# Values of the retention heads transposed by DMA as two 16-bit planes, and an order for ScalarE behind the second quad

## The chip, the cores and the metric

The kernel runs on one core of a Trainium2 chip. The metric is the time of one execution on the device in microseconds (us); the kernel is run several times and the median is given. The engines are TensorE (PE, with its weight loads as PEld), VectorE (DVE), ScalarE (ACT), GpSimd (POOL) and SyncE (SP), whose queue here issues all the transfers; 16 DMA engines carry them out.

## The reference

A decoder layer of 2048 positions and width 1024 with 16 learned meta tokens ahead of them. After an RMS norm, one projection gives eight groups of 512 columns. Four of them feed a gated short convolution, four (Q, K, V and a gate RG) feed four retention heads of width 128, computed in chunks of 128 positions:

```python
hn = rms_norm(h, norm_g)
cx, cb, cc, cg, q, k, v, rg = jnp.split(hn @ w_in, 8, axis=-1)
conv_out = short_conv(cx, cb, cc) * silu(cg)
scores = einsum('bhnid,bhnjd->bhnij', qc, kc) * decay
inner = einsum('bhnij,bhnje->bhnie', scores, vc)
upd = einsum('bhnjd,bhnje->nbhde', kc * zeta, vc)      # summed over positions
states: s = chunk_decay * s + upd                      # carried from chunk to chunk
cross = einsum('bhnid,nbhde->bhnie', qc * xi, states)
ret = head_group_norm(inner + cross) * silu(rg)
out = rms_norm(h + concat(conv_out, ret) @ w_out)
```

Both `inner` and `upd` sum over positions of a chunk, so V is needed with positions in the partitions. The projection leaves it with the head's 128 columns in the partitions.

## The kernel before

The 2048 positions are taken in two halves of 1024 (r = 0 and 1), each half in two blocks of 512 (j = 0 and 1). A half runs through eight units: 0 to 3 are the retention heads (`head`), 4 to 7 the convolution groups; the first half begins with group 4, then come heads 0 to 3. After both halves, `output` makes eight pairs of row tiles with the output projection.

Each unit has two quads of projections. A quad multiplies a 2x2 block of weights by a 2x2 block of activations in seven products instead of eight (`quad`); every factor is split into a high and a low part (`wh`, `wl` for weights, `mh`, `ml` for activations), so a product is 12 matmuls of 128x512. Products share banks of PSUM (`pj`): ACT copies a bank to `tc` after products 0, 2 and 3, and `take(i, j, bank, c)` hands the results over in the order (0,0), (1,1), (0,1), (1,0); the last one has no copy to be added. The weights of a quad are four loads `ra`; `stationary` builds the sums on POOL (first `sa`, of the last two loads, then three in place), casts on ACT (`wh`) and subtracts on DVE (`wl`), in a ring of three. The first quads of the program and the first of head 0 in the second half are plain ones of eight products (`quad_plain`), which hand over K and V of one j together.

A head's first quad gives K and V. K goes through `rotary` on DVE; V of j = 1 comes as the sum of a bank and a copy on DVE (L587 of the listing, shown as L110 in rows), V of j = 0 as a plain copy by ACT (L585). The second quad gives Q and RG. Then, for each j: four transposes of K on PE (L631) into a bank `ms`, scaled by ACT into `kd` (L633); four transposes of V on PE (L636) into another `ms`, scaled by four instructions of ACT, one a chunk, back into V's tile (L640); four update matmuls (L646) and four state updates on DVE (L649). Later stand the scores (L659), the two matmuls of the output (L669, L670), statistics on DVE, the power `rp` on POOL (L682), `pm` on DVE (L686), four transposes on PE (L693) and the store to `mixed` (L444).

Beside the heads run other pieces. After heads 1 and 2 of the first half, `prepare` makes the block sums of the second half's activations (`x`, L174 and L177, stored as `sums_x`); in the second half it does the same for the output weights. `prepared` loads these sums again as `t` (L200): eight of them between the two quads of head 0 in the second half, for products 3 and 4 of its second quad. `meta_state` loads a small table `mr` (L415) and sets the head's first state from the meta tokens (`mk`, L403, L425).

The order of instructions on each engine is set by the framework's scheduler, not by the order of the code alone; all transfers go through SP's queue in its order. Tiles named `kv`, `qg`, `x`, `t` come from one pool of 16 buffers (`gen`).

Of the kernel before, what the change touches and what calls it, by code (L numbers as in the profile page):

```python
# [8 lines left out]
F32 = mybir.dt.float32  # L9
F32R = mybir.dt.float32r  # L10
BF16 = mybir.dt.bfloat16
AF = mybir.ActivationFunctionType
ALU = mybir.AluOpType

P = 128
# [6 lines left out]
HB = 512  # L22
NR = 2
BLK = SEQ // NR
CH = HB // P
# [45 lines left out]
def hybrid_trunk(ctx: ExitStack, tc: tile.TileContext, t, out: bass.AP, chunk_decay):  # L71
# [5 lines left out]
    nc = tc.nc  # L77
# [11 lines left out]
    def ps_misc():  # L89
        return ps.tile([P, HB], F32, name="ms", tag="ms", bufs=4)  # L90

    def gen(name="g"):
        return sb.tile([P, HB + 16], F32, name=name, tag="g", bufs=GEN)[:, : 2 + HB]
# [99 lines left out]
    def prepared(m, src, ns, held={}):  # L193

        for n in ns:
            for kt in range(KH):
# [3 lines left out]
                    nc.sync.dma_start(a, src[n, kt])  # L200
                parts(m, SUMS[n], kt, a)

    def quad(w, m, take):


        def product(i, bank, first):
            (wh, wl) = w[i]
            for kt in range(KH):
                ks = slice(kt * P, (kt + 1) * P)
                mh, ml = m[i][kt]  # L210
                for n, (a, b) in enumerate(((wl, mh), (wh, ml), (wh, mh))):
                    nc.tensor.matmul(  # L212
                        bank, a[:, ks], b, start=first and kt == 0 and n == 0, stop=kt == KH - 1 and n == 2,
                        skip_group_check=not first,
                    )

        def copy(bank):
            c = sb.tile([P, HB], F32, name="tc", tag="tc", bufs=COPIES)
            nc.scalar.copy(out=c, in_=bank)  # L219
            return c  # L220

        xb = ps_proj()
        product(0, xb, True)
        c = copy(xb)
        yb = ps_proj()
        product(1, yb, True)
        take(0, 0, yb, c)
        product(2, xb, False)
        u2 = copy(xb)
        zb = ps_proj()  # L230
        product(3, zb, True)
        c = copy(zb)
        product(4, xb, False)
        take(1, 1, xb, c)
        product(5, zb, False)
        take(0, 1, zb, u2)
        product(6, xb, False)
        take(1, 0, xb, None)
# [61 lines left out]
    ident = const.tile([P, P], F32, name="ident")  # L300
# [265 lines left out]
    def rotary(a, table):  # L566
# [5 lines left out]
        nc.vector.tensor_tensor(out=a, in0=a, in1=table[:, 0, :], op=ALU.mult)  # L572
        turned[0] = nc.vector.tensor_tensor(out=a, in0=a, in1=rot[:, :w], op=ALU.add)

    def head(h, r, m, rot_t, f, blocks, ahead, first=(), between=()):


        between = iter(between)
        k, v = [None, None], [None, None]
        tables = [rot_t[:, :, j * HB : (j + 1) * HB] for j in range(2)]  # L580

        def take(i, j, pp, c):
            d = gen("kv")[:, :HB]
            if c is None:
                nc.scalar.copy(out=d, in_=pp)  # L585
            else:
                add(nc.vector, d, pp, c)  # L587
            if i == 0:
                rotary(d, tables[j])
                k[j] = d  # L590
            else:
                v[j] = d

        if len(first) > 0:
            quad_plain(first[0], m, take)
# [29 lines left out]
        blocks = ahead()  # L625
        states = [state[h]]
        vt = []
        for j in range(2):
            tp = ps_misc()
            for c in range(CH):  # L630
                nc.tensor.transpose(tp[:, c * P : (c + 1) * P], k[j][:, c * P : (c + 1) * P], ident)  # L631
            kd = brief("kd")
            nc.scalar.mul(kd, tp, kd_col[:, h : h + 1])  # L633
            tp = ps_misc()
            for c in range(CH):
                nc.tensor.transpose(tp[:, c * P : (c + 1) * P], v[j][:, c * P : (c + 1) * P], ident)  # L636
            vj = v[j]
            for c in range(CH):
                cs = slice(c * P, (c + 1) * P)
                nc.scalar.mul(vj[:, cs], tp[:, cs], f[2][j][0][:, c : c + 1])  # L640
            vt.append(vj)
            last = r == NR - 1 and j == 1
            up = ps_misc()
            for c in range(CH - last):
                cs = slice(c * P, (c + 1) * P)
                nc.tensor.matmul(up[:, cs], kd[:, cs], vj[:, cs], start=True, stop=True)  # L646
            for c in range(CH - last):
                nxt = sb.tile([P, P], F32, name="state", tag="state", bufs=2 * CH)
                nc.vector.scalar_tensor_tensor(  # L649
                    out=nxt, in0=states[-1], scalar=chunk_decay[h], in1=up[:, c * P : (c + 1) * P],  # L650
# [4 lines left out]
        for j in range(2):  # L655
            sc = ps_misc()
            for c in range(CH):
                cs = slice(c * P, (c + 1) * P)
# [245 lines left out]
```

## Time and profile before

| | |
|---|---|
| time, median of 3 runs | 894.16 us (893.94 to 894.59) |
| profiled execution, its own time | 893.76 us |
| its span on the profile | 892.0 us |
| PE busy | 879.8 us, 99% |
| DVE busy | 717.7 us, 80% |
| ACT busy | 407.2 us, 46% |
| POOL busy | 397.8 us, 45% |
| moved by DMA | 116.94 MB, 131 GB/s on the mean |

The busy times are sums over instructions of one profiled execution. Matmuls overlap each other, so the mean time of one (some 390 ns for 128x512) is longer than its step from one to the next. A row of a timeline gives the start and the length of an instruction, or of several alike in a row (x4), with the idle time ahead of it and what ended it in brackets. Line numbers in rows are those of the kernel before; additions and subtractions made through the helpers show the helpers' lines (L110, L113), and casts L101.

### The profile page before, as it was taken

What the parts mean: (1) busy time and instruction counts of PE and PEld (TensorE: products, weight loads), DVE (VectorE), ACT (ScalarE), POOL (GpSimd) and SP (SyncE); (2) the same over time, 40 slices, a digit from 0 to 9 for tenths busy, and PEclk for the clock granted to TensorE, in tenths of its full rate; (3) what the DMA queues carried; (4) which work ended last, traced back from release to release, by engine and by line L of the source; (5) the groups of instructions that cost most, each with busy time, mean ns of one, the idle gap of its engine ahead of it and who ended that gap; (6) DMA issues with size and microseconds to landing.
All of it is one profiled execution on the core that took longest, in us unless ns stands there. A gap on an engine that the chain in (4) does not pass through costs nothing.

```text
span 892.0 us, 12867 instructions
## 1 busy us (share of the span) xinstructions
PE 879.8 (99%) x4407; PEld 725.0 (81%) x4407; DVE 717.7 (80%) x1176; ACT 407.2 (46%) x816; POOL 397.8 (45%) x291
## 2 busy tenths in 40 slices
PE   8999999999999999999999999999999999999996
PEld 5778788888888778888888888888888888788885
DVE  6788887988967966999889899777668699766764
ACT  8674424234245364746243332423333476545553
POOL 0554222313134654452323323345546454787773
PEclk9999999999999999999999999999999999999999
DMA  9711224354224252834135272313131393555532
GB/s 336 231 65 48 72 54 150 129 159 149 73 83 142 83 154 75 293 117 141 48 95 200 71 245 87 96 58 95 49 93 49 117 390 101 183 165 160 183 121 81
DMA packets 76242, 116.94 MB, mean 131 GB/s; under 512 B 7632, under 2 KB 24336, under 8 KB 76176
## 3 DMA queue, kind: packets, MB, share of 16 engines
q1 hardware_dynamic: 76176, 116.11, 40.3%
q8 instruction: 35, 0.57, 0.3%
q14 instruction: 31, 0.25, 0.1%
HBM read 90.92 MB, written 25.17 MB: 130 GB/s over the span
## 4 chain that ended last, share of the span: by engine, by line
PE 82%; DVE 8%; DMA 4%; issue 2%; ACT 2%; POOL 2%; SPq 0%; POOLq 0%; DVEq 0%; ACTq 0%
PE pj L212 66%; PE pj L262 6%; DVE ml L113 2%; PE ms L669 1%; PE ms L670 1%; PE ms L659 1%; PE ms L646 1%; DMA w<-in_w_out 1%; DMA ra<-in_w_in 1%; PE ms L397 1%; DVE wl L113 1%; PE ms L693 1%; DVE ml L105 1%; PE ms L631 1%; PE ms L636 1%
## 5 line engine op out<-in xcount | busy, mean ns | idle before, releaser
L212 PE MATMUL pj<-mh,wl 128*128 128x512 f32 x1008 | 399.1, 396 | 1.5 <-ACT wh L101 0.6
L212 PE MATMUL pj<-ml,wh 128*128 128x512 f32 x1008 | 393.3, 390 | 0.0
L212 PE MATMUL pj<-mh,wh 128*128 128x512 f32 x1008 | 393.0, 390 | 0.0
L101 ACT CAST wh<-ra 128x512 fp32r<-128x512 f32 x216 | 134.0, 621 | 311.0 <-PE pj L212 264.9
L212 PEld LDWEIGHTS pj<-mh,wl 128*128 128x128 f32 x1008 | 189.4, 188 | 43.2 <-issue 2.2
L113 DVE TENSOR_TENSOR wl<-ra,wh 128x512 fp32r<-128x512 f32 x216 | 194.1, 899 | 34.5 <-ACT wh L101 34.0
L212 PEld LDWEIGHTS pj<-mh,wh 128*128 128x128 f32 x1008 | 189.2, 188 | 39.9
L212 PEld LDWEIGHTS pj<-ml,wh 128*128 128x128 f32 x1008 | 189.5, 188 | 37.8 <-issue 0.5
L113 POOL TENSOR_TENSOR ra<-ra 128x512 f32<-128x512 f32 x72 | 112.8, 1566 | 84.1 <-DVE qg L614 32.3
L110 POOL TENSOR_TENSOR sa<-ra 128x512 f32<-128x512 f32 x36 | 54.9, 1526 | 120.6 <-DVE wl L113 53.1
L113 POOL TENSOR_TENSOR ra<-sa,ra 128x512 f32<-128x512 f32 x36 | 52.0, 1444 | 92.6 <-DVE wl L113 89.1
L219 ACT COPY tc<-pj 128x512 f32<-128x512 f32 x108 | 62.7, 580 | 0.0
L262 PE MATMUL pj<-ml,mh 128*128 128x512 f32 x128 | 50.2, 392 | 0.1
L262 PE MATMUL pj<-mh,mh 128*128 128x512 f32 x128 | 49.9, 392 | 0.0
L262 PE MATMUL pj<-mh,ml 128*128 128x512 f32 x128 | 48.7, 397 | 0.7 <-DVE ml L113 0.6
L682 POOL TENSOR_TENSOR rp<-rs,neg_half 128x4 f32<-128x4 f32 x16 | 19.9, 1246 | 48.1 <-DVE rs L110 47.8
L723 DVE TENSOR_TENSOR yo<-pj,yo 128x512 f32<-128x512 f32 x32 | 21.9, 686 | 17.6 <-PE pj L212 7.8
L101 ACT CAST wh<-sa 128x512 fp32r<-128x512 f32 x36 | 22.4, 621 | 29.1 <-PE pj L212 28.9
L522 POOL TENSOR_TENSOR c<-c,rr 128x512 f32<-128x512 f32 x14 | 26.1, 1865 | 19.6 <-DVE c L459 9.6
L686 DVE TENSOR_SCALAR pm<-ms,mv,rp 128x128 f32<-128x128 f32 x64 | 21.9, 404 | 15.8 <-POOL rp L682 15.8
L522 POOL TENSOR_TENSOR c<-c,tc 128x512 f32<-128x512 f32 x14 | 26.1, 1862 | 18.7 <-ACT tc L548 18.7
L728 POOL TENSOR_TENSOR z<-yo,final_g 128x512 f32<-128x512 f32 x16 | 26.9, 1682 | 15.9 <-DVE yo L723 15.9
(137 smaller groups left out, 1145.5 us busy)
## 6 DMA issues: line engine op xcount, KB each, us to landing
ra<-in_w_in SPq DMA_DIRECT2D x128, 256.0 KB, 2.7
x<-in_xT SPq DMA_DIRECT2D x48, 256.0 KB, 4.8
w<-in_w_out SPq DMA_DIRECT2D x32, 256.0 KB, 5.2
ra<-mixed SPq DMA_DIRECT2D x32, 256.0 KB, 2.6
yo<-in_x SPq DMA_DIRECT2D x32, 256.0 KB, 4.5
ra<-in_x SPq DMA_DIRECT2D x16, 256.0 KB, 3.2
mixed<-c SPq DMA_DIRECT2D x16, 256.0 KB, 2.6
mixed<-qg SPq DMA_DIRECT2D x16, 256.0 KB, 2.3
```

Source lines behind the costliest of these rows:

```text
L101: nc.scalar.copy(out=hi, in_=src)
L105: nc.vector.scalar_tensor_tensor(out=lo, in0=src, scalar=scale, in1=hi.bitcast(F32), op0=ALU.mult, op1=ALU.subtract)
L110: eng.tensor_tensor(out=out, in0=a, in1=b, op=ALU.add)
L113: eng.tensor_tensor(out=out, in0=a, in1=b, op=ALU.subtract)
L212: nc.tensor.matmul(bank, a[:, ks], b, start=first and kt == 0 and n == 0, stop=kt == KH - 1 and n == 2, skip_group_check=not first,)
L219: nc.scalar.copy(out=c, in_=bank)
L262: nc.tensor.matmul(banks[i], a[:, ks], b, start=half + kt + n == 0, stop=half == 1 and kt == KH - 1 and n == 2,)
L522: eng.tensor_tensor(out=out, in0=a, in1=b, op=ALU.mult)
L682: nc.gpsimd.tensor_tensor(out=rp, in0=rs, in1=neg_half.rearrange("p (c a) -> p c a", a=1), op=ALU.pow)
L686: nc.vector.tensor_scalar(out=y[:, cs], in0=o[:, cs], scalar1=mv[:, c, 0:1], scalar2=rp[:, c, :], op0=ALU.subtract, op1=ALU.mult,)
L723: last[0] = nc.vector.tensor_tensor(out=y, in0=pp, in1=y, op=ALU.add)
L728: nc.gpsimd.tensor_tensor(out=ys[i][j], in0=y, in1=final_g[:, j * HB : (j + 1) * HB], op=ALU.mult)
```

## The change

V isn't transposed by PE any more. `turn` makes a copy on ACT that sets the upper and lower 16-bit halves of each of the 128x512 values apart, as two planes side by side (`pl`), and a DMA transposes the 1024 16-bit columns in blocks of 128 (`tr`). For V of j = 0 that copy reads the bank and takes the place of the plain copy; for j = 1 it reads the sum that DVE made. After the second quad, `whole` copies the halves together again (`wo`), and the four scalings work in place on that tile. These copies and scalings are issued under `issue_after` of the last bank copy of the second quad (`copied`). The head's transposes of K, its updates and all that follows read as before, with `wo` in the place of `kv`.

```diff
@@ -200,6 +201,8 @@
                     nc.sync.dma_start(a, src[n, kt])
                 parts(m, SUMS[n], kt, a)
 
+    copied = [None]
+
     def quad(w, m, take):
 
 
@@ -216,7 +219,7 @@
 
         def copy(bank):
             c = sb.tile([P, HB], F32, name="tc", tag="tc", bufs=COPIES)
-            nc.scalar.copy(out=c, in_=bank)
+            copied[0] = nc.scalar.copy(out=c, in_=bank)
             return c
 
         xb = ps_proj()
@@ -572,6 +575,27 @@
         nc.vector.tensor_tensor(out=a, in0=a, in1=table[:, 0, :], op=ALU.mult)
         turned[0] = nc.vector.tensor_tensor(out=a, in0=a, in1=rot[:, :w], op=ALU.add)
 
+    def halves(a):
+        return a.bitcast(U16).rearrange("p (n two) -> p two n", two=2)
+
+    def planes(a):
+        return a.bitcast(U16).rearrange("p (two n) -> p two n", two=2)
+
+    def turn(a):
+
+
+        apart, across = gen("pl")[:, :HB], gen("tr")[:, :HB]
+        nc.scalar.copy(out=planes(apart), in_=halves(a))
+        nc.sync.dma_start(
+            across.bitcast(U16).rearrange("p (c f) -> p c f", c=2 * CH), apart.bitcast(U16), transpose=True
+        )
+        return across
+
+    def whole(across):
+        a = gen("wo")[:, :HB]
+        nc.scalar.copy(out=halves(a), in_=planes(across))
+        return a
+
     def head(h, r, m, rot_t, f, blocks, ahead, first=(), between=()):
 
 
@@ -580,6 +604,9 @@
         tables = [rot_t[:, :, j * HB : (j + 1) * HB] for j in range(2)]
 
         def take(i, j, pp, c):
+            if i == 1 and c is None:
+                v[j] = turn(pp)
+                return
             d = gen("kv")[:, :HB]
             if c is None:
                 nc.scalar.copy(out=d, in_=pp)
@@ -589,7 +616,7 @@
                 rotary(d, tables[j])
                 k[j] = d
             else:
-                v[j] = d
+                v[j] = turn(d)
 
         if len(first) > 0:
             quad_plain(first[0], m, take)
@@ -625,19 +652,19 @@
         blocks = ahead()
         states = [state[h]]
         vt = []
+        with tc.issue_after(copied[0].ins):
+            for j in range(2):
+                v[j] = whole(v[j])
+                for c in range(CH):
+                    cs = slice(c * P, (c + 1) * P)
+                    nc.scalar.mul(v[j][:, cs], v[j][:, cs], f[2][j][0][:, c : c + 1])
         for j in range(2):
             tp = ps_misc()
             for c in range(CH):
                 nc.tensor.transpose(tp[:, c * P : (c + 1) * P], k[j][:, c * P : (c + 1) * P], ident)
             kd = brief("kd")
             nc.scalar.mul(kd, tp, kd_col[:, h : h + 1])
-            tp = ps_misc()
-            for c in range(CH):
-                nc.tensor.transpose(tp[:, c * P : (c + 1) * P], v[j][:, c * P : (c + 1) * P], ident)
             vj = v[j]
-            for c in range(CH):
-                cs = slice(c * P, (c + 1) * P)
-                nc.scalar.mul(vj[:, cs], tp[:, cs], f[2][j][0][:, c : c + 1])
             vt.append(vj)
             last = r == NR - 1 and j == 1
             up = ps_misc()
```

The numbers of lines after the change are 3 higher around L400 to L450 and 27 higher behind L600: L660 is the scaling of V (L640 before), L666 the one of K, L673 the update, L676 the state, L589 the DMA transpose, L596 the copy back, L222 the bank copy, L102, L111 and L114 the helpers' lines. The order of the instructions moves in three places that matter for what follows.

ACT, at the end of head 1's second quad in the first half, from the meta state to the first casts of the next unit. Before:

```order
L425 COPY state_83<-ms 128x128
L615 ACTIVATE qg<-qg 128x512
L403 COPY mk<-ms 16x128 x4
L633 ACTIVATE kd<-ms,cols 128x512
L640 ACTIVATE kv<-ms,rc_400 128x128 x4
L177 ACTIVATE x<-x,gain 128x512
L101 CAST wh<-ra 128x512
L101 CAST wh<-sa 128x512
L219 COPY tc<-pj 128x512
```

Now, the same stretch:

```order
L428 COPY state_83<-ms 128x128
L596 COPY wo<-tr 128x2x512 x2
L642 ACTIVATE qg<-qg 128x512
L406 COPY mk<-ms 16x128 x4
L660 ACTIVATE wo<-wo,rc_400 128x128 x4
L666 ACTIVATE kd<-ms,cols 128x512
L178 ACTIVATE x<-x,gain 128x512
L660 ACTIVATE wo<-wo,rc_440 128x128 x4
L102 CAST wh<-ra 128x512
L102 CAST wh<-sa 128x512
L222 COPY tc<-pj 128x512
```

The two copies back stand ahead of the last silu; the scalings of the first block come before `kd`, those of the second before the casts for the third product of the next stretch.

DVE at the same place, from the meta sums to the low weights of the next products. Before:

```order
L110 TENSOR_TENSOR mk<-mk 16x128 x2
L174 SCALAR_TENSOR_TENSOR x<-x,gain 128x512
L113 TENSOR_TENSOR wl<-ra,wh 128x512
L174 SCALAR_TENSOR_TENSOR x<-x,gain 128x512
L113 TENSOR_TENSOR wl<-sa,wh 128x512
L174 SCALAR_TENSOR_TENSOR x<-x,gain 128x512
L113 TENSOR_TENSOR x<-x 128x512
```

Now:

```order
L111 TENSOR_TENSOR mk<-mk 16x128 x2
L175 SCALAR_TENSOR_TENSOR x<-x,gain 128x512 x3
L676 SCALAR_TENSOR_TENSOR state<-state_83,ms 128x128
L114 TENSOR_TENSOR x<-x 128x512
L114 TENSOR_TENSOR wl<-ra,wh 128x512
L114 TENSOR_TENSOR wl<-sa,wh 128x512
```

The first `wl` stood behind one of the block sums `x`; it stands behind three of them, a state update and one more `x` now.

SP's queue, at head 0 of the second half (behind the stores of a convolution group) up to the loads of the prepared sums. Before:

```order
L444 DMA mixed_89<-c 128x4x128
L444 DMA mixed_88<-c 128x4x128
L436 DMA ra<-in_w_in 128x512
L200 DMA t<-sums_x 128x512 x8
L436 DMA ra<-in_w_in 128x512 x7
```

Now:

```order
L447 DMA mixed_89<-c 128x4x128
L447 DMA mixed_88<-c 128x4x128
L589 DMA_TRANSPOSE tr<-pl 128x8x128
L439 DMA ra<-in_w_in 128x512
L589 DMA_TRANSPOSE tr<-pl 128x8x128
L201 DMA t<-sums_x 128x512 x8
L439 DMA ra<-in_w_in 128x512 x7
```

The eight loads `t` stand behind both transposes now.

## Rows read from the trace of the kernel before

**Rows 1.** Page: busy time by engine; granted clock of PE in tenths, 40 slices

```profile
PE 879.8 (99%) x4407; PEld 725.0 (81%) x4407; DVE 717.7 (80%) x1176; ACT 407.2 (46%) x816; POOL 397.8 (45%) x291
...
PEclk9999999999999999999999999999999999999999
```

**Rows 2.** Waits of PE: line, releaser, us in total, times, longest

```profile
PE ms L766 <- ACT warm L760: 2.3, 1, 2.3
...
PE pj L212 <- DVE wl L113: 0.2, 1, 0.2
```

**Rows 3.** Groups of instructions by shape: busy us, mean ns, idle before

```profile
L636 PE MATMUL ms<-ident,kv 128*128 128x128 f32 x64 | 10.2, 273 | 0.0
...
L219 ACT COPY tc<-pj 128x512 f32<-128x512 f32 x108 | 62.7, 580 | 0.0
...
L403 ACT COPY mk<-ms 16x128 f32<-16x128 f32 x32 | 8.1, 254 | 2.0 <-PE ms L397 1.6
...
L649 DVE SCALAR_TENSOR_TENSOR state<-state,ms 128x128 f32<-128x128 f32 x60 | 16.9, 282 | 4.2 <-PE ms L646 3.3
```

**Rows 4.** Chain of waits in 195 to 208: start us, us, what

```profile
200.19 5.49 PE pj L212 x24
...
207.01 0.44 PE ms L636 x4
```

**Rows 5.** Timeline of ACT, head 1: start us, us, what [idle before <-releaser]

```profile
174.50 0.59 ACT L585 COPY kv<-pj 128x512 f32<-128x512 f32 x1 [2.10 <-PE pj L212]
...
199.17 0.63 ACT L615 ACTIVATE qg<-qg 128x512 f32<-128x512 f32 x1 [3.85 <-DVE qg L614]
...
201.38 1.13 ACT L640 ACTIVATE kv<-ms,rc 128x128 f32<-128x128 f32 x4
```

**Rows 6.** Timelines of DVE and PE, head 1 of the first half

```profile
168.43 0.68 DVE L110 TENSOR_TENSOR kv<-pj,tc 128x512 f32<-128x512 f32 x1
...
203.15 1.15 DVE L174 SCALAR_TENSOR_TENSOR x<-x,gain 128x512 f32<-128x512 f32 x1 [1.93 <-ACT x L177]
204.22 0.68 DVE L113 TENSOR_TENSOR wl<-ra,wh 128x512 fp32r<-128x512 f32 x1
204.82 0.74 DVE L174 SCALAR_TENSOR_TENSOR x<-x,gain 128x512 f32<-128x512 f32 x1
...
207.20 0.48 PE L212 MATMUL pj<-mh,wl 128*128 128x512 f32 x1
```

**Rows 7.** Timelines of SP, POOL, DVE and PE, same head

```profile
178.06 0.33 SPq L436 DMA_DIRECT2D ra<-in_w_in  x1
...
181.33 1.27 POOL L110 TENSOR_TENSOR sa<-ra 128x512 f32<-128x512 f32 x1 [4.59 <-DVE wl L113]
187.10 1.40 POOL L682 TENSOR_TENSOR rp<-rs,neg_half 128x4 f32<-128x4 f32 x1 [4.50 <-DVE rs L110]
...
188.54 1.37 DVE L686 TENSOR_SCALAR pm<-ms,mv,rp 128x128 f32<-128x128 f32 x4 [0.91 <-POOL rp L682]
...
191.10 0.60 PE L693 MATMUL ms<-ident,pm 128*128 128x128 f32 x4
```

**Rows 8.** DMA issues (KB, us to landing); a window (PEclk, DMA share, GB/s last)

```profile
mixed<-qg SPq DMA_DIRECT2D x16, 256.0 KB, 2.3
...
181.00:183.00 2.00, 2.00 (x19) 1.96 (x18) 1.86 (x3) 0.62 (x1) 1.27 (x1) 1.00 0.45 133
```

**Rows 9.** Timelines of ACT, SP, DVE and PE, head 0, second half

```profile
402.74 1.27 ACT L585 COPY kv<-pj 128x512 f32<-128x512 f32 x2 [3.64 <-PE pj L262]
...
400.79 3.27 SPq L200 DMA_DIRECT2D t<-sums_x  x7
...
409.41 2.59 DVE L113 TENSOR_TENSOR ml<-t,mh 128x512 fp32r<-128x512 f32 x2
...
412.25 0.39 PE L212 MATMUL pj<-mh,wl 128*128 128x512 f32 x1
```

**Rows 10.** A window: us, busy of PE, PEld, DVE, ACT, POOL, and more

```profile
470.00:520.00 50.00, 49.68 (x259) 41.89 (x258) 45.52 (x83) 15.60 (x29) 17.85 (x12) 1.00 0.44 140
```

More of the change, by code (lines that the diff above doesn't have):

```diff
@@ L11 @@
 BF16 = mybir.dt.bfloat16
+U16 = mybir.dt.uint16
 AF = mybir.ActivationFunctionType
```

## The prediction

> **What bounds the kernel now.** I read the engines' shares first: TensorE (PE) is busy for 879.8 of 892.0 us, at a granted clock of nine tenths or more all along (2.4 GHz, the upper of its two levels) [rows 1]. The waits of PE come next: seven groups, from 2.3 at the start of the program down to 0.2, 4.7 in all [rows 2]. So nothing can be won from waiting. A change gains by taking work from PE, and loses where it makes PE wait; PE has next to no waits in which a new one could vanish. ScalarE (ACT) is busy 46%, VectorE (DVE) 80% of the mean, which hides stretches in which it is as full as PE: from 470 to 520 it works 45.5 of 50 us [rows 10].
>
> **What is removed.** PE's part of the transposes of V: 64 instructions of 128x128 at line 636. Their busy time, 10.2 us [rows 3], is not their price, since matmuls overlap. The price is their pace in the chain: a group of four takes 0.44 [rows 4], 0.11 each. 64 x 0.11 = **7.0 us** off PE. The bank of PSUM and the read of it by ACT go too; nothing waits for these today [rows 2].
>
> **What is added on ACT.** Per head two copies to 16-bit planes and two back. No row has a copy with a stride of 16 bits. From 254 ns for 128 elements in a row and 580 for 512 [rows 3], each further element costs 0.85 ns, so 1024 halves are about 1.02 us. Bounds: 0.58, if a pair of halves goes as one element, and 1.6, if the stride costs as much again on top. I take 1.02, nearest to the two rows. 8 heads x 4 = 32 copies, 33 us; gone are the 9 plain copies of V among line 585's eleven (two are K's, in the head whose first quad is the plain one), 9 x 0.59 [rows 5], so ACT gains some 27 us and stands near 49%. What counts is where. The copy to planes of the last product starts where the plain copy did, at 174.50 in head 1, and delays the cast behind it by 0.4 [rows 5]. The copies back fall, by the order of issue shown above, into ACT's 3.85 us of idling before 199.17 [rows 5]: 2.04 in 3.85, **nothing**, as long as the transposes have landed by 197. Without that cover they would push the casts that feed PE, 2 us a head.
>
> **What moves: DVE at the third product.** This is the cost that the added work doesn't show. In head 1 the third product starts at 207.20, and its low weights (wl) were made by DVE at 204.22, one place behind the first of the block sums (x) [rows 6]. In the order now, three x, a state update (L676) and another x stand ahead of that wl. From 203.15: 1.1 + 0.7 + 0.7 (the x, by their starts [rows 6]) = 205.6; the state update needs the update matmuls, which end 0.44 earlier than before, near 205.6, and takes 0.28 [rows 3]; the x 0.6 (by the starts); then wl 0.68. So PE gets it at about 207.1, where its own work would let it start at 207.2 - 0.87 = 206.3. Of the 0.87 freed there, 0.1 is left, and with the cast of that weight, which ACT now does behind four more scalings (1.13 [rows 5]), none, or 0.2 less than none: I take a loss of 1.0. Heads 1 and 2 of the first half have this shape, since the sums are prepared there: **+2.0**. In head 0 PE waits for a wl of DVE already, behind the second group of V's transposes, which is the one wait of 0.2 for wl [rows 2], so that group's 0.44 isn't gained: **+0.4**.
>
> **What moves: the queue of SP.** Every transfer is issued by SP in order, so two transposes a head come ahead of other loads. No row shows a DMA transpose. Bounds from the store of a head's output, 256 KB in 512-byte pieces: landing 2.3; in its two microseconds the 16 DMA engines are busy 0.45, so 0.9 us of all of them for 512 pieces, 28 ns of one engine a piece [rows 8]; an issue holds SP 0.33 [rows 7]. A transpose moves the same 256 KB in 1024 pieces of 256 bytes (128 partitions x 8 blocks): 0.9 us if bytes decide, 1.8 if pieces do, 28.7 if one engine after the other took a piece; and SP is held 0.33 (one issue) up to 8 x 0.33 = 2.6 (one for each of eight blocks). I take 1.8, the price by the piece, since such small pieces are what the store's row shows.
> In heads 1 to 3 the pair is ready at about 170.1 (168.43 + 0.68 + 1.02) and 175.5 (174.50 + 1.02) [rows 5, 6], and the load behind it went out at 178.06 [rows 7]: hidden.
> In head 0 of the second half it isn't. There V's second half is turned after the copies of 402.74, at 404.4, and eight loads t of the prepared sums, which went out from 400.79, now stand behind it [rows 9]. They come 404.4 + 1.8 - 400.8 = 5.4 later. The fourth of them is split by about 410.7 (half of the pair from 409.41) and is wanted three steps of 3 x 0.229 after the third product's start at 412.25, at 414.3 [rows 9, 4]; so 3.6 of it is covered: **+1.8** (0.9 by bytes; 2.6 with SP held 2.6).
>
> **DVE-bound heads.** In heads 1 to 3 of the second half DVE has 4.5 us of idling in 50 [rows 10], more than the 0.87 that PE would run ahead in each; between 0 and 3 x 0.87 = 2.6 I take **+0.4**, near the lower end, as wl's lead over PE there is not used up in any listed wait.
>
> **Sum.** -7.0 + 2.0 + 0.4 + 1.8 + 0.4 = -2.4. The profiled run of before took 893.76 (span 892.0 and 1.8 around it), so about 891.4; the median of the three runs is 0.4 above that run, so **891.8**, 0.26% faster. The span should be near 889.6.
>
> **A rule weighed.** The rows bear only on plain transfers. The Trainium skill, "Advanced Engine Details and Errata", section "X-Bar Transpose (TRN2)", says that transpose DMAs are as fast as regular ones, at about 90% of a copy; by that the 0.9 of bytes holds and the sum is -3.3. The same skill, "VectorE: DVE Perf Modes", section "The three transpose paths", speaks against the change: 390 ns for TensorE and 1309 for a DMA on a 128x128 block; eight blocks in a row would be an estimated 10.5 us, rival 2. No row of before decides between them.
>
> **Rivals.**
> 1. *All of it is gained.* If DVE's order does no harm (the block sums wait for nothing and ACT is early) and the t loads are early enough: 893.76 - 7.0 + 0.4 = 887.1. For: PE waits for almost nothing today. Against: the DVE rows of 203 to 207, which leave 0.1. Chance 0.07.
> 2. *The transposes hold the queue: slower.* Ten us each, a third of the bound of 28.7, in order: 170.1, 180.1, 190.1, and the load behind lands at 190.1 + 2.3 = 192.4. Its block goes to POOL's sum at 181.33 today, which in POOL's order stands ahead of rp (187.10), and DVE and then the transposes of PE at 191.10 wait for rp [rows 7]. 192.4 + 1.3 + 1.4 + 1.4 = 196.5 against 191.1: 5.4 a head, six heads (1 to 3 of each half) 32. The t loads: 414.4 or later against 400.8, less 3.6, 10. Sum -7 + 32 + 10 = +35: **about 929**. It decides where the pair ends later than about 185, that is from some 7 us a transpose; the t loads alone turn the sum at about 4 (2.4 more than taken). Chance 0.20.
> 3. *Middling prices: nothing gained.* A transpose of 2.5 to 6 us adds 0.7 to 4.2 at the t loads; copies of 1.6 instead of 1.02 add 0.6 there, and where half of the heads pass one such delay on to a cast, 2.4. With 3 us for these, 895; 892.4 to 900. Chance 0.28, of it 0.16 within 0.2% and 0.12 above.
> My own case has 0.45: its range is 889.5 to 894, by 0.9 to 2.8 us a transpose and 0 to 2.6 in the DVE-bound heads; three quarters of it lie below 892.4.
>
> **How the numbers follow.** A run of this kernel can tell a difference of 0.2%, 1.8 us, from none: faster is below 892.4, slower above 895.9. Faster: 0.07 + 0.35 = 0.42; within: 0.10 + 0.16 = 0.26; slower: 0.20 + 0.12 = 0.32. The range: 887 at the full gain; above, it takes in rival 3 and the nearest prices of rival 2 (7 to 8 us), 905, and leaves 0.18 out.
>
> **What would show it.** PE's busy time should fall by about 10 and its waits rise by 4 to 5: a wait for wl near 206 to 207 in heads 1 and 2, and one for ml of t in head 0 of the second half, each with DVE named. ACT's copies to planes should read about 1.0 us, its copies back lie in the gap before the silu. The rows of DMA issues give the transposes' landing: 2 to 3.5 us is my case; 5 or more, rival 2 or 3, with PE's waits at rp's users (pm, L686 of before) and SP's next load far behind the plane copy. Copies well above 1.6, or PE waiting for the scaled values at the updates (L646 of before), would make my sum wrong in a way that no rival has.

## The result, and the profile after

The changed kernel is slower: 897.99 us on the median of 7 runs (896.12 to 898.97) against 894.59 (893.94 to 895.06), a ratio of 1.0036 with a 95% interval of 1.0024 to 1.0047. Forecast was 891.8 with a range of 887 to 905, so the time lies in the range and the direction was wrong.

The traces differ more than the medians: the profiled run of before, 893.76, lies 0.8 below its median, and the one of after, 898.97, 1.0 above. Of the 5.2 us between the spans, 1.8 belongs to that; two waits that differ between traces without a moved instruction are named below.

Page of the kernel after, busy time by engine (answers to rows 1):

```profile
span 897.2 us, 12769 instructions
...
PE 876.2 (98%) x4343; PEld 718.6 (80%) x4343; DVE 718.5 (80%) x1176; ACT 436.9 (49%) x839; POOL 396.3 (44%) x291
...
PEclk9999999999999999999999999999999999999999
```

PE has its 64 instructions less and is on the same clock, but its waits, 4.7 us in all before [rows 2], are 13.5 now. Waits of PE in the kernel after (line, releaser: us in total, times, longest):

```profile
PE pj L215 <- ACT kd L666: 2.5, 2, 1.2
PE ms L793 <- ACT warm L787: 2.3, 1, 2.3
PE pj L215 <- ACT tc L222: 2.1, 4, 1.2
PE pj L215 <- DVE ml L114: 1.9, 1, 1.9
PE pj L215 <- ACT wh L102: 1.8, 2, 1.1
PE ms L720 <- DVE pm L713: 0.9, 1, 0.9
PE pj L265 <- DVE ml L114: 0.7, 1, 0.7
PE ms L295 <- DVE rot L288: 0.6, 1, 0.6
PE ms L427 <- DVE mk L111: 0.4, 1, 0.4
PE pj L215 <- DVE wl L114: 0.3, 1, 0.3
```

The idle time in such rows begins where the matmul ahead is modelled to end. Measured from start to start (a step of 0.23 for 128x512, 0.11 in the banks ms, 0.03 from one to the other, all else is waiting) the main places are these; the three columns are worked out from the starts of PE's rows in the traces of before, after and the best version found below:

| place | before | after | best |
|---|---|---|---|
| first unit, a bank copy at 63 to 64 (L215) | 0.7 | 1.4 | under 0.2 |
| head 0, first half, third product behind | 0.5 | 1.4 | 1.4 |
| head 1, first half | 0 | 1.5 | 0 |
| head 2, first half | 0 | 1.5 | 1.6 + 1.2 |
| head 3, first half | 0 | 0 | 0 |
| head 0, second half, second quad | 0 | 2.9 | 0 |
| heads 1 to 3, second half | 0 | 3 x 0.55 | 0.3 |
| transposes near 606 (L720) | 0 | 1.1 | 1.1 |
| output, first plain quad (L265) | 0.2 | 0.8 | 0.2 |

By this table PE waits 10.9 more than before and does 7.0 less, 3.9 in sum; the medians differ by 3.4. Head 3 is what was hoped for everywhere: its two groups of transposes go, two steps are 0.44 shorter each, and PE does not wait at its third product.

The new work by shape, and the DMA transposes, in the kernel after (busy us, mean ns; for the DMA the hold of the queue in ns and the landing in us):

```profile
L596 ACT COPY wo<-tr 128x1024 uint16<-128x1024 uint16 x16 | 20.7, 1360 | 0.0
...
L588 ACT COPY pl<-pj 128x1024 uint16<-128x1024 uint16 x9 | 9.1, 1012 | 18.0 <-PE pj L215 17.9
...
L588 ACT COPY pl<-kv 128x1024 uint16<-128x1024 uint16 x7 | 7.3, 1047 | 6.3 <-DVE kv L111 6.3
...
L589 SPq DMA_TRANSPOSE tr<-pl x16: 1232/1239/1358, 74.9 to 548.5; - x16
...
DMA to landing us min/median/max: 2.7/3.1/4.3
```

The copies to planes cost what was worked out (1.01 for 1.02), the copies back a third more (1.36 for 1.02). A transpose holds SP 1.24 us, where a plain load holds it 0.33 [rows 7], and lands 3.1 us after its issue, where the plain store takes 2.3 [rows 8]. Of the two rules of the Trainium skill that the prediction weighed, the one in "Advanced Engine Details and Errata", section "X-Bar Transpose (TRN2)" (as fast as a regular DMA), is the nearer one, though a third too good here (3.1 against 2.3); eight times the 1309 ns of "VectorE: DVE Perf Modes", section "The three transpose paths", is not what eight blocks in one DMA take here.

### The profile page after: what moved, and what is told of

It is laid out like the page before. It is cut to its first block, busy times and chain, and to the rows that moved or that the text cites. A ratio compares the mean times of both kernels' runs of the same rounds, so it can differ in the third digit from the quotient of the medians.

```text
span 897.2 us, 12769 instructions
## 1 busy us (share of the span) xinstructions
PE 876.2 (98%) x4343; PEld 718.6 (80%) x4343; DVE 718.5 (80%) x1176; ACT 436.9 (49%) x839; POOL 396.3 (44%) x291
## 5 line engine op out<-in xcount | busy, mean ns | idle before, releaser
L215 PE MATMUL pj<-mh,wl 128*128 128x512 f32 x1008 | 399.3, 396 | 6.9 <-ACT kd L666 2.5
L215 PE MATMUL pj<-ml,wh 128*128 128x512 f32 x1008 | 393.0, 390 | 1.9 <-DVE ml L114 1.9
L215 PE MATMUL pj<-mh,wh 128*128 128x512 f32 x1008 | 393.5, 390 | 0.0
L102 ACT CAST wh<-ra 128x512 fp32r<-128x512 f32 x216 | 133.7, 620 | 289.1 <-PE pj L215 232.2
L215 PEld LDWEIGHTS pj<-mh,wl 128*128 128x128 f32 x1008 | 189.4, 188 | 50.2 <-ACT tc L222 5.8
L114 DVE TENSOR_TENSOR wl<-ra,wh 128x512 fp32r<-128x512 f32 x216 | 194.6, 903 | 39.9 <-ACT wh L102 39.3
L215 PEld LDWEIGHTS pj<-ml,wh 128*128 128x128 f32 x1008 | 189.4, 188 | 40.4 <-DVE ml L114 2.3
L215 PEld LDWEIGHTS pj<-mh,wh 128*128 128x128 f32 x1008 | 189.2, 188 | 39.9
L114 POOL TENSOR_TENSOR ra<-ra 128x512 f32<-128x512 f32 x72 | 112.0, 1555 | 82.7 <-DVE qg L641 31.2
L111 POOL TENSOR_TENSOR sa<-ra 128x512 f32<-128x512 f32 x36 | 54.0, 1501 | 124.3 <-DMA ra<-in_w_in 33.6
L114 POOL TENSOR_TENSOR ra<-sa,ra 128x512 f32<-128x512 f32 x36 | 51.6, 1433 | 98.9 <-DVE wl L114 95.5
L222 ACT COPY tc<-pj 128x512 f32<-128x512 f32 x108 | 62.5, 579 | 0.0
L265 PE MATMUL pj<-ml,mh 128*128 128x512 f32 x128 | 50.3, 393 | 0.1
L265 PE MATMUL pj<-mh,mh 128*128 128x512 f32 x128 | 50.0, 393 | 0.0
L265 PE MATMUL pj<-mh,ml 128*128 128x512 f32 x128 | 49.0, 399 | 0.7 <-DVE ml L114 0.7
L102 ACT CAST wh<-sa 128x512 fp32r<-128x512 f32 x36 | 22.2, 617 | 26.6 <-PE pj L215 26.6
```

The source lines that it names most:

```text
L102: nc.scalar.copy(out=hi, in_=src)
L111: eng.tensor_tensor(out=out, in0=a, in1=b, op=ALU.add)
L114: eng.tensor_tensor(out=out, in0=a, in1=b, op=ALU.subtract)
L215: nc.tensor.matmul(bank, a[:, ks], b, start=first and kt == 0 and n == 0, stop=kt == KH - 1 and n == 2, skip_group_check=not first,)
L222: copied[0] = nc.scalar.copy(out=c, in_=bank)
L265: nc.tensor.matmul(banks[i], a[:, ks], b, start=half + kt + n == 0, stop=half == 1 and kt == KH - 1 and n == 2,)
```

## The experiments

Theory A was that the loss is ACT's longer work ahead of casts and bank copies, and the late t loads; B, that the DMA transposes lose it by holding SP and the DMA engines; C, that other places of the program take the saving back whatever the work. D and E, below, split A: the row of scalings on ACT, and the block sums on DVE.

Times are medians; the ratio is to the kernel before, run on the same chip in the same rounds, with its 95% interval.

| run | us | ratio | |
|---|---|---|---|
| e4_bare | 891.39 | 0.9965 (0.9953 to 0.9978) | no transpose, no copies |
| e12_bare_late | 892.24 | 0.9978 (0.9968 to 0.9988) | same, scalings behind K's |
| e3_no_dma | 895.33 | 1.0006 (0.9997 to 1.0015) | copies, no DMA |
| e5_dma_only | 895.57 | 1.0011 (1.0002 to 1.0020) | before, with idle DMA transposes |
| e7_head0 | 895.66 | 1.0012 (1.0004 to 1.0021) | one head back on PE |
| e1_free | 898.95 | 1.0049 (1.0035 to 1.0063) | without the order behind the bank copy |
| e10_late | 896.30 | 1.0020 (1.0011 to 1.0029) | scalings behind K's |
| e11_late_head0 | 893.12 | 0.9990 (0.9981 to 0.9998) | e10 and e7 |
| e21_t_first_only | 895.49 | 1.0014 (1.0005 to 1.0023) | t loads first |
| **e17_late_t_first** | **891.66** | **0.9969 (0.9957 to 0.9982)** | e10 and e21 |
| e14_before_sums | 899.07 | 1.0050 (1.0037 to 1.0063) | before, sums in the convolution groups |
| e15_sums | 897.82 | 1.0044 (1.0028 to 1.0059) | after, same |
| e13_sums_late_head0 | 899.75 | 1.0055 (1.0043 to 1.0068) | e11, same |
| e16_t_first | 897.02 | 1.0032 (1.0020 to 1.0044) | e17, same |
| e20_before_behind | 900.39 | 1.0066 (1.0053 to 1.0078) | before, sums behind the states |
| e19_after_behind | 900.30 | 1.0068 (1.0056 to 1.0081) | after, same |
| e18_behind | 899.36 | 1.0057 (1.0045 to 1.0070) | e17, same |

**What each part costs.** Three kernels take the change apart. e4_bare, against the changed kernel:

```diff
-            if i == 1 and c is None:
-                v[j] = turn(pp)
-                return
...
-                v[j] = turn(d)
+                v[j] = d
...
-                v[j] = whole(v[j])
```

> The change without its price: V is neither transposed nor copied to planes; the eight scalings run in place on the untransposed tile, after the last bank copy, so that the output is not the reference's. Theory A (what was lost is ACT's longer work, standing ahead of casts and bank copies, plus the late t loads): nothing of either is left, so the full 7.0 us should show, 887.5 to 888.5 us. Theory B (the DMA transposes, by holding SP and the DMA engines, lose it): the same here. Theory C (any other order of the program loses some us, whatever the work): well above 889.

Measured 891.39, 3.2 us below before and not 7.0. So more than half of PE's saving does not show although nothing was added. The trace (span 889.6) says where; its waits of PE:

```profile
...
PE ms L692 <- DVE pm L684: 1.7, 2, 1.2
PE pj L215 <- ACT tc L222: 1.7, 2, 0.9
PE pj L215 <- ACT kd L662: 0.7, 1, 0.7
PE pj L265 <- DVE ml L114: 0.7, 1, 0.7
...
```

PE comes sooner to `pm` of heads 1 and 2 (0.7 and 1.4 of waiting, start to start; DVE is at work there without a pause) and to the third product behind head 0 (0.5 more than before), and finds them not ready: 2.6. Another 1.9 stands outside the heads: 0.4 more than before at the first unit, 0.9 at a bank copy at 679 and 0.6 more at the output. That the saving causes these is not shown: the first of them lies ahead of the first V, and waits like them stand in kernels in which PE saves nothing (first unit and output in e5_dma_only, a bank copy at 687 in e14_before_sums, both below).

e12_bare_late puts the scalings of each block behind its scaling of K (the diff is that of e10_late below):

> V neither transposed nor copied (the output is not the reference's), with each block's scalings behind its scaling of K. It took 891.4 with all eight scalings in a row. Theory D: the row of eight was what kept 3.7 of the 7.0 us from showing: 888 to 889. Rival (the place of other work, at the first unit and the output, keeps them): 891.

Measured 892.24: no better, so it isn't the row of eight scalings that keeps the saving. The waits only change their names (3.3 us for wl, 2.6 for the scaled values). Theory C, that other places take the saving back, holds for about half of the 7.0.

e3_no_dma puts the copies back but no transpose:

```diff
-        apart, across = gen("pl")[:, :HB], gen("tr")[:, :HB]
+        apart = gen("pl")[:, :HB]
...
-        nc.sync.dma_start(
-            across.bitcast(U16).rearrange("p (c f) -> p c f", c=2 * CH), apart.bitcast(U16), transpose=True
-        )
-        return across
+        return apart
```

> The changed kernel without its 16 DMA transposes: the copies to planes and back stay, and the copy back reads the planes themselves, so V is not transposed and the output is not the reference's. Theory A: only the 2.9 us at the t loads of head 0 in the second half come back, 898.0 - 2.9 = 895. Theory B: most of the loss comes back, 888 to 890.

Measured 895.33, as theory A had it: the copies cost 895.3 - 891.4 = 3.9, the transposes 898.0 - 895.3 = 2.7 (differences of medians). The 3.9 is not the time of the copies alone; with them instructions stand in another order. In e4_bare DVE has the old order at head 2, one block sum ahead of the first `wl`, and PE waits for nothing at the third products behind heads 1 and 2, where it waits 1.5 each with the copies:

```profile
202.08 0.77 DVE L175 SCALAR_TENSOR_TENSOR x<-x,gain 128x512 f32<-128x512 f32 x1 [0.95 <-ACT x L178]
202.98 1.56 DVE L114 TENSOR_TENSOR wl<-ra,wh 128x512 fp32r<-128x512 f32 x1
```

The wait of 1.1 near 606 is of this kind too; it stands in every kernel here that has the copies and in none without. PE's transposes wait there for `pm`, which needs the statistics. Before, DVE made the statistics ahead of a product of the convolution group (`tc<-tc,rr`):

```profile
599.09 0.88 DVE L675 BATCH_NORM_STATS2 st<-ms 128x6 f32<-128x128 f32 x4
...
602.37 0.68 DVE L522 TENSOR_TENSOR tc<-tc,rr 128x512 f32<-128x512 f32 x1
```

In the kernel after it makes them behind that product, and POOL makes `rp` behind the next piece of the group:

```profile
604.56 1.78 DVE L525 TENSOR_TENSOR tc<-tc,rr 128x512 f32<-128x512 f32 x1
606.26 0.88 DVE L702 BATCH_NORM_STATS2 st<-ms 128x6 f32<-128x128 f32 x4
...
608.47 1.02 POOL L709 TENSOR_TENSOR rp<-rs,neg_half 128x4 f32<-128x4 f32 x1
```

The converse, e5_dma_only, has in the kernel before, behind `v[j] = d`:

```diff
+                across = gen("tr")[:, :HB]
+                nc.sync.dma_start(
+                    across.bitcast(U16).rearrange("p (c f) -> p c f", c=2 * CH), d.bitcast(U16), transpose=True
+                )
```

> The kernel before, with the 16 DMA transposes added and their results unused: each reads V's tile as raw halves; PE transposes V as before. Theory A: SP's hold of 16 x 1.24 us costs only what stands behind it at the t loads, some 2 to 3 us: about 897. Theory B: 6 us or more: above 900.

Measured 895.57, 0.9 us more than before: 16 holds of 1.24 us on SP cost at most that, theory B is out, and theory A's 897 was too high as well. The loads t stand behind both transposes here too, 4.5 later than before with the lateness of the whole kernel (0.3) taken off, and PE waits only 0.5 for them. So a lateness of about 4 is covered at this place:

```profile
405.64 3.90 SPq L201 DMA_DIRECT2D t<-sums_x  x8
```

This run also shows that two waits need not come from the change. At the first unit's bank copy and at the output every engine has its instructions in the order of before, no V is handed over ahead of the first place, and yet the trace has there waits like those of the kernel after, and the profiled run of before has smaller ones [rows 2]:

```profile
...
PE pj L213 <- ACT tc L220: 0.8, 1, 0.8
PE pj L263 <- DVE ml L114: 0.7, 1, 0.7
...
```

What makes them longer or shorter from one trace to the next is open.

**The transposes' place.** e7_head0 does head 0 of the second half as before (`v[j] = turn(d) if not (r == 1 and h == 0) else d`, and PE's transposes under the opposite condition):

> The changed kernel with head 0 of the second half as in the kernel before (V transposed by PE there, no DMA transposes ahead of the t loads), the other seven heads changed. Theory A: 2.9 us at the t loads come back and 0.87 of PE's gain is given up: 898.0 - 2.0 = 896. Theory B: one eighth of the loss, within 1 us of the changed kernel, 897 to 898.

Measured 895.66, as theory A had it. e21_t_first_only leaves that head to the DMA and only issues its pair later: in this head `turn` puts the transfer into a list, which is sent behind the loads.

```diff
-                v[j] = turn(d)
+                v[j] = turn(d, waiting)
...
         next(between, lambda: None)()
+        for send in waiting or ():
+            send()
```

> The changed kernel with the two transposes of head 0 in the second half issued behind the t loads, nothing else. If their place costs what PE waited there (2.2 + 0.2 + 0.5), 898.0 - 2.9 = 895. If the gain of 4.6 that the same step gave on top of the other order of the scalings is its own, 893.5. If it was only the two together, 897.

Measured 895.49, 2.5 below the changed kernel: that place was nearly all of the DMA's 2.7. The loads on SP before:

```profile
400.79 3.75 SPq L200 DMA_DIRECT2D t<-sums_x  x8
```

SP's timeline in the kernel after, and PE's wait:

```profile
401.79 1.29 SPq L589 DMA_TRANSPOSE tr<-pl  x1
...
406.68 1.25 SPq L589 DMA_TRANSPOSE tr<-pl  x1
407.98 4.85 SPq L201 DMA_DIRECT2D t<-sums_x  x8
...
418.03 0.50 PE L215 MATMUL pj<-ml,wh 128*128 128x512 f32 x1 [1.94 <-DVE ml L114]
```

The loads are 7.2 later than before, of which the kernel as a whole was 2.2 late by then; and the eight of them took 4.85 to issue, not 3.75, since one issue was held for 1.5 us. The last of them is thus 6 late, more than the 4 that e5_dma_only shows to be covered.

**The row of scalings.** e1_free takes the order behind the last bank copy away and nothing else:

> The changed kernel without the order behind the last bank copy, nothing else. In the first half ACT's order stays the same, so theory D expects no change there; in the second half the scalings and copies back may go ahead of bank copies. Theory D: 898, within 1 us. Rival (that order is what costs): 895 or less.

Measured 898.95: nothing gained, as theory D had it; the same waits stand in its trace. e10_late moves the scalings:

```diff
-                for c in range(CH):
-                    cs = slice(c * P, (c + 1) * P)
-                    nc.scalar.mul(v[j][:, cs], v[j][:, cs], f[2][j][0][:, c : c + 1])
...
-            nc.scalar.mul(kd, tp, kd_col[:, h : h + 1])
+            behind = nc.scalar.mul(kd, tp, kd_col[:, h : h + 1])
             vj = v[j]
+            with tc.issue_after(behind.ins):
+                for c in range(CH):
+                    cs = slice(c * P, (c + 1) * P)
+                    nc.scalar.mul(vj[:, cs], vj[:, cs], f[2][j][0][:, c : c + 1])
```

> The changed kernel with the four scalings of each block of positions issued on ACT behind that block's scaling of K, as in the kernel before; the copies back stay behind the last bank copy. Theory D (what ACT's copies cost is not their time but the eight scalings in one row ahead of the casts and bank copies of the next unit): the waits of 1.36, 1.48 and 1.48 at heads 0 to 2 and of 0.55 at heads 1 to 3 of the second half shrink by most, some 4.5 us of 6.0: 893.5. Rival (ACT's added time itself is in the way, wherever the scalings stand): the waits move, 897 or more.

Measured 896.30, 1.7 below the changed kernel, less than half of what was expected. The three waits of 0.55 in the second half are gone; there the row of eight stood ahead of a bank copy that PE waited for. ACT's timeline in the kernel after, and PE:

```profile
479.13 2.44 ACT L660 ACTIVATE wo<-wo,rc 128x128 f32<-128x128 f32 x8
481.47 0.60 ACT L102 CAST wh<-sa 128x512 fp32r<-128x512 f32 x1
481.98 0.57 ACT L222 COPY tc<-pj 128x512 f32<-128x512 f32 x1
...
482.61 0.50 PE L215 MATMUL pj<-mh,wl 128*128 128x512 f32 x1 [0.30 <-ACT tc L222]
```

Head 1's wait is gone too, heads 0 and 2 keep theirs (1.3 each), and two new ones of 0.8 came, for `pm` at head 2 and at head 1 of the second half. Head 1 alone got back the old order on DVE (one block sum ahead of the first wl, not three), which points to DVE.

**The block sums on DVE.** In the kernel after, head 2 of the first half; DVE, ACT and PE:

```profile
205.56 2.58 DVE L175 SCALAR_TENSOR_TENSOR x<-x,gain 128x512 f32<-128x512 f32 x3 [2.07 <-ACT x L178]
208.42 0.29 DVE L676 SCALAR_TENSOR_TENSOR state<-state,ms 128x128 f32<-128x128 f32 x1 [0.28 <-PE ms L673]
208.62 0.68 DVE L114 TENSOR_TENSOR x<-x 128x512 f32<-128x512 f32 x1
209.23 0.69 DVE L114 TENSOR_TENSOR wl<-ra,wh 128x512 fp32r<-128x512 f32 x1
...
206.60 0.60 ACT L102 CAST wh<-ra 128x512 fp32r<-128x512 f32 x1
...
207.33 1.05 PE L673 MATMUL ms<-wo,kd 128*128 128x128 f32 x8
...
210.06 0.47 PE L215 MATMUL pj<-mh,wl 128*128 128x512 f32 x1 [1.24 <-ACT kd L666]
```

ACT has the cast done at 207.2; DVE has made wl of it only at 209.9, when three sums, a state and a fourth sum are done. The three sums ended at 208.1; the state behind them had to wait for PE's own update matmuls (L673, to 208.4), and from there the state, the fourth sum and wl take the 1.5 that PE waits. The view names `kd`, which ended at the same 209.92; a wait for several semaphores is put down to the last one. e15_sums prepares the sums after convolution groups 5 and 6, and e14_before_sums does so in the kernel before:

```diff
-                if unit > 0:
+                if unit > 0 and r > 0:
...
+                if r == 0 and unit in (5, 6):
+                    next(later, None)
+                    next(later, None)
```

> The kernel before, with the block sums of the second half's activations (x) prepared after convolution groups 5 and 6 of the first half instead of after heads 1 and 2. PE waits for nothing at heads 1 and 2 in the kernel before, so every theory expects no gain: 894.5, within 1 us. A gain of over 1.5 us here would say that the move is worth it by itself, and the two runs with it below would have to be read against this one.

> The changed kernel with the same move of the block sums, nothing else. Theory E (at heads 1 and 2 PE waits because the sums on DVE stand ahead of the low weights, as the prediction had it): the two waits of 1.48 go, 898.0 - 2.9 = 895. Rival, theory D for these heads (the eight scalings on ACT hold the cast of the same weight): the cast comes no earlier, most of the waits stay, 897 or more.

The move is dear by itself, which no theory had: 899.07, since PE waits in those groups (1.5 us for `mk` and 1.2 for a sum on DVE in e14's trace). e15_sums took 897.82. By that number alone the rival would hold; against its base it loses nothing any more (1.3 less, with intervals that overlap), where in the old place the change loses 3.4. What decides is the trace: the wait follows the sums. In e15, DVE at head 1, which has no sums ahead of wl now, and at head 3, beside which the first of them were put:

```profile
154.48 0.69 DVE L114 TENSOR_TENSOR wl<-ra,wh 128x512 fp32r<-128x512 f32 x1 [3.14 <-ACT wh L102]
...
252.09 2.58 DVE L175 SCALAR_TENSOR_TENSOR x<-x,gain 128x512 f32<-128x512 f32 x3 [0.77 <-DMA rot_t<-in_rot]
254.91 0.29 DVE L676 SCALAR_TENSOR_TENSOR state<-state,ms 128x128 f32<-128x128 f32 x1 [0.25 <-PE ms L673]
255.12 0.68 DVE L114 TENSOR_TENSOR x<-x 128x512 f32<-128x512 f32 x1
255.72 0.68 DVE L114 TENSOR_TENSOR wl<-ra,wh 128x512 fp32r<-128x512 f32 x1
...
256.55 0.47 PE L215 MATMUL pj<-mh,wl 128*128 128x512 f32 x1 [1.24 <-ACT kd L666]
```

Behind heads 1 and 2, with ACT's scalings still in front of the casts, PE waits for nothing; behind head 3, where it waited for nothing, it has the 1.24 to the digit. So theory E holds for these waits, not D.

e20_before_behind and e19_after_behind leave the sums in the heads, behind the last state update:

```diff
-                if unit > 0:
+                if unit > 0 and r == 0:
+                    with tc.issue_after(updated[0].ins):
+                        next(later, None)
+                        next(later, None)
...
```

> The kernel before, with the block sums of heads 1 and 2 issued on DVE behind the last state update of their head, so that the low weights of the next unit come first. PE waits for nothing there, so all theories: 894.6, within 0.7 us.

> The changed kernel with the same order of the block sums, nothing else. Theory E (DVE's sums ahead of the low weights are what PE waits for at heads 1 and 2): the waits of 1.48 and 1.48 go, 898.0 - 2.9 = 895. Theory D for these heads (the row of scalings on ACT holds the cast): the waits stay above 1, 897 or more.

Neither came out: 900.39 and 900.30. The sums held back cost 5.9 us of themselves (in e20 the updates of heads 2 and 3 wait 3.2 us of it for V's scalings), which I had put at nothing. All that these two say is that on this base the change costs nothing; they do not decide between E and D.

**Together.** e11_late_head0 is e10 with e7's head, e17_late_t_first e10 with e21's order:

> The last one, with head 0 of the second half by PE as in the kernel before. Theory D with the late t loads: both gains add, 893.5 - 2.3 = 891. Rival: as the kernel with that head alone, 895.7.

> The changed kernel with the scalings of each block behind its scaling of K, and the two transposes of head 0 in the second half issued behind the t loads. Against the same without the latter (896.3): if the place ahead of the t loads is all they cost there, the waits of 2.6 go, 893.7; if the transposes are then late for their users, 895 or more.

Measured 893.12 (between theory and rival) and 891.66 (2.0 better than expected). The second beats both kernels: 2.8 us below before, all heads by DMA. Its waits of PE:

```profile
...
PE pj L215 <- DVE wl L114: 1.6, 2, 1.4
PE ms L707 <- DVE pm L699: 1.2, 2, 1.1
PE pj L215 <- ACT wo L678: 1.1, 1, 1.1
PE ms L731 <- DVE pm L724: 0.9, 1, 0.9
...
```

The two steps gave 1.7 and 2.5 alone and 6.3 together. From the trace of e10 to that of e17 2.4 us go at the loads t, and 1.2 at the first unit and 0.6 at the output, where neither step moved an instruction. So part of the 6.3, and of the 2.8 below before, need not come from the steps; why these two waits are short in this kernel is open.

The three with the sums elsewhere, e13_sums_late_head0, e16_t_first and e18_behind, were to show that nothing else is left:

> Changed kernel with the scalings of each block behind its scaling of K, head 0 of the second half by PE, and the block sums moved: theories D and E and the late t loads taken together. It took 893.1 without the move. Theory E: the waits of 1.6 and 1.2 that were left at head 2 go, 890.5. Rival (the transposes and copies cost in other places what is saved): 892.5 or more.

> As the last one, but all eight heads by DMA, with the two transposes of head 0 in the second half issued behind the eight t loads instead of ahead of them. If the place ahead of the t loads is all that the DMA costs in that head, this head gains its 0.87 as well: about 1 us below the last one, 889.6. Rival (the weight loads behind the pair are late instead, or its result is): as the last one or slower.

> The last one, with the block sums behind the last state update as well: all causes named so far are taken away. Theory (these are all): waits of 1.3 at head 0 and 1.1 near 606 are left, 894.6 - 7.0 + 1.0 + 1.1 + 1 = 890.7. Rival (the saving on PE is taken back wherever DVE or ACT are near their limit): 892.5 or more.

They took 899.75, 897.02 and 899.36. The move's own price (a wait of 6.0 us for `mk` of a convolution group in the first two; 2.2 us at each of two heads in the third) hides what they were to show. e16 is 2.7 below e13; in the traces 1.3 of that stands at the first unit and the output again, so that the DMA serves head 0 better than PE is not shown by it. Head 2 without its sums ahead, at no cost elsewhere, was not found.

## Why the prediction was wrong

It saw the right kinds of cost at the places that it read, but it counted all of PE's saved work as saved time. The experiments give the sum in the prediction's own parts. Forecast was -7.0 for PE, +2.8 for what the copies move on DVE (2.0, 0.4 and 0.4, with ACT itself at nothing) and +1.8 for SP: -2.4. Measured was -3.2 (e4_bare), +3.9 (e3_no_dma) and +2.7 (the transposes): +3.4. The second point rests on a row of before that the sum did not use, PE's update matmuls at head 2:

```profile
205.52 1.05 PE L646 MATMUL ms<-kv,kd 128*128 128x128 f32 x8
```

- **PE's saving of 7.0**: right as work (0.44 a group, seen at head 3), wrong as time. e4_bare shows 3.2, and these 3.8 are most of the miss. The step that failed is "PE has next to no waits in which a new one could vanish": an engine that never waits may still have nothing ready ahead of it. What was late next was counted in heads 0 to 2 and at the t loads only; `pm` (2.1 in e4_bare at heads 1 and 2) and the bank copies were not looked at. For 1.9 of it, outside the heads, the cause is open.
- **DVE at the third product**: mechanism and place right, size not. Forecast was a loss of 1.0 in each of heads 1 and 2; measured was 1.5 of waiting each, 3.0 against 2.0, so that heads 1 and 2 came out 0.6 and 0.7 slower. The mis-sized term is the end of the update matmuls, which the prediction put near 205.6. Their row of before ends at 206.6, with 0.44 off at 206.1. From there the prediction's own chain (state, x, wl) ends at 207.7, 1.4 behind PE's 206.3. The cast on ACT, the other term of that loss, was done early. The rows at 168 to 208 that are called head 1 there are those of head 2; head 1 has the same rows 50.4 us earlier, so the sum is not touched by that. Head 0: 0.4 forecast, 0.9 more seen, and still there in e10 and e17; its cause is open.
- **SP and the t loads**: 1.8 forecast, 2.5 (e21) to 2.9 (trace). The price of a transpose was well placed, 1.24 and 3.1 between the bounds of 0.33 to 2.6 and of 0.9 to 28.7, and the cover of 3.6 fits the 4 or so of e5; the eight loads themselves going out slower by 1.1 was not foreseen.
- **ACT**: "nothing" failed. The copies back do lie in the idle stretch as forecast, but eight scalings in a row, now free of PE's transposes, come ahead of the next unit's casts and bank copies. For the first half the order rows showed it; for heads 1 to 3 of the second half no rows were read, and 3 x 0.55 stands there. The prediction put 0.4 on these heads for DVE. The 1.1 near 606, where the order on DVE and POOL moved, was not in it at all.
- **Signs**: the wait for ml and the transposes' landing came as said. PE's busy time fell by 3.6, not by 10 (busy times of overlapping matmuls don't add up), and its waits rose by 8.8, not by 4 to 5.
- **Rivals**: the nearest was the third, middling prices at 892.4 to 900, but not for its reasons; transposes and copies were in their expected bounds. The second needed 7 us a transpose and is out by the landing of 3.1 and by e5. A rival was missing in which the price is as taken and PE's saving is given back at several places. That 897.99 lies inside the range is luck: its upper part was there for slow transposes, which did not come.

## What to carry to other kernels

Where one engine is busy 99% and waits for nothing, read how early its partners are before you count its saved work as time: the lead of each operand, at each place behind the saving. A kernel with the work simply left out gives that bound in one run. A transfer that is cheap by itself costs by what stands behind it in its queue, and small work set free from a wait on PE can run ahead of what PE needs; tying it to its old place gave 1.7 here. New work on one engine can also change the order on others: compare the order on every engine, at every place, before and after.

## What was not expected of the hardware

A copy that writes 16-bit halves two apart costs ACT 1.36 us for 1024 elements; one that reads them two apart costs 1.01 from a bank of PSUM and 1.05 from a tile of SBUF. A DMA transpose of 128x1024 16-bit elements holds the issuing queue 1.24 us, nearly four times the 0.33 of a plain transfer of the same 256 KB. Eight plain loads right behind a transpose took 3.90 us to issue in e5_dma_only, hardly more than the 3.75 of before, but 4.85 in the kernel after, where the first of them held the queue for 1.53; why is open.
